# A two-layer hybrid diffusion backbone on one core: the instruction scheduler orders by another estimate of time

## The chip, the cores and the metric

The kernel runs on one core of one Trainium2 chip. The core has five engines with an instruction queue each: TensorE (PE; its weight loads are shown apart as PEld), VectorE (DVE), ScalarE (ACT), GpSimd (POOL) and SyncE (SP), which here issues the loads of weights. The metric is the device time of one execution in microseconds (us), lower is better. The kernel before took 2425.48 us as the median of three runs (2423.67 to 2432.31).

## The reference

256 latent tokens and 256 context tokens of width 1024 go through two layers. Each layer has a mixer of three parallel branches (a Mamba-2 state-space branch in both directions, here SSD; a neighbourhood attention; a Conformer convolution), merged by gates, and a feed-forward part, dense in the first layer and with the best two of eight experts in the second. Both parts are modulated by vectors (adaLN) that are products of a conditioning vector with `ada_w`. All data are float32. Cut to its core:

```
for layer in range(2):
    mod_l = split(silu(c) @ ada_w[layer] + ada_b[layer], 6)       # mod_c from c_ctx
    h_l = modulate(rms_norm(x, norm_mix[layer]), mod_l[0], mod_l[1])
    h_c = modulate(rms_norm(ctx, norm_mix[layer]), mod_c[0], mod_c[1])
    y_l, y_c = token_mixer(h_l, h_c, lp, need_ctx)
    x = x + mod_l[2] * y_l
    h_l = modulate(rms_norm(x, norm_ffn[layer]), mod_l[3], mod_l[4])
    ...
    f_all = swiglu(h_all, ...) if layer == 0 else moe_swiglu(h_all, ...)
    x = x + mod_l[5] * f_all[:, n_ctx:]
return rms_norm(x, final_norm)

def ssd_scan(xs, dt, a, bm, cm, h0):                     # chunks of 128 positions
    decay = exp(where(lower, cs_t[..., :, None] - cs_t[..., None, :], -inf))
    y_diag = einsum('bcgls,bcgels,bcsgep->bclgep', scores, decay, xd)
    y_off = einsum('bclgn,bcgepn,bclge->bclgep', cm, h_in, exp(cs))
    return y_diag + y_off, h_last
```

## The kernel before

**Weights.** Every matrix comes in units of 128x1024 floats (512 KB). `raw` (L119) loads one on SP's queue. `split` makes two numbers of each weight for PE: ACT copies it to a shorter format (L114, the tile h_...), DVE subtracts that from the original (L115, the tile l_...). The activations are split in the same way, and a product is the sum of three, h by H, h by L and l by H (L179, L180, L181 in `wstat`; L226 to L228 in `wmov`). In the mixers three raw buffers and two of each split turn, in the expert loop six and three.

**The mixers** (`mix`). A loop goes over the parts `glu dt qkv xbc g1 ssd p1 g2 p2 z g0 p0` (layer 1: z before p2). g0 to g2 are the gates (tiles wg), z the SSD's gate (zL), p0 to p2 the projections of the branches (wb0ssd_out, wb0na_out, wb0conf_out). Other jobs run in the background: attention, the convolution, the SSD, and the adaLN blocks. They are Python generators; after each weight unit `pump` lets each of them emit some instructions, at a rate. So weight matmuls (fillers) lie in the source between the short steps of these jobs.

**The SSD's end** (`ssd_y`, `ssd_norm`). For a chunk and half of the heads, four groups: `cbS` (L975, PE turns four columns), ACT makes the decays `MS` of it (L978, L979), DVE masks them (L980), PE multiplies (`ydS`, L983). Then `peS` and `yoS` (L996, L997), ACT and DVE on `ES` (L1000 to L1005), and `uL` (L1008). At the end of a layer eight products with z (L932), squares (L934), row sums on PE (`rcyS`, L779), the reciprocal (`rryS`, L787 on DVE, L788 on POOL) and its broadcast on PE (`rbyS`, L791).

**adaLN on DVE** (`ada_v`). 20 blocks; for each, eight tiles `adaw` of 128x512 are loaded on SP (L339) into two buffers and multiplied and summed on DVE (`adac`, L343 for the first, L345 for the others, once or twice for each tile). PE sums over the partitions (`ada`, L350), DVE adds the bias (L351). The twelve blocks of layer 1 run beside the dense feed-forward part of layer 0.

**The experts** (`moe`, `expert`, `stream`). Eight experts, gate and up (eg, eu) and down (ed); r in a name (egr, eur, edr) marks the stream of the sorted tokens. Which expert is next SP reads from memory (L1340), a count from L1224. In the second half two experts' streams run in turn. After each 512 columns a short transpose (L1354) and ACT and DVE steps follow.

**What sets the order.** The instructions of all engines are emitted by the source and then put in order by the scheduler of the tile framework, before the program is compiled: it runs over the instructions with an estimate of when each engine is free and when its inputs are ready, and takes what is ready by priority. The source shifts priorities: `prio` wraps work into `high_priority` with the offsets of `PR` (weights 10000, evacuations, attention, SSD and adaLN 5000, norms 20000, start 30000, `lg` -20000). Each engine then works through its own list in order. The framework is entered in `kernel`, at L1573:

## Time and profile before

| | |
|---|---|
| median of three runs | 2425.48 us (2423.67 to 2432.31) |
| the profiled execution | 2422.2 us, span 2420.4 us |
| granted TensorE clock, mean of the span | 0.988 |
| PE busy, PEld busy | 2317.3 us (96%), 1807.8 us (75%) |
| DVE busy, ACT busy | 1852.8 us (77%), 1338.4 us (55%) |
| loaded by DMA | 469.68 MB, mean 194 GB/s; 326 to 357 GB/s in the expert loop |
| L115 `l_eur`, `l_edr`, `l_egr` on DVE | 154 each, 1.22 us |
| L345 `adac` on DVE | 224, 0.75 us; 54.8 us idle before it |

Busy times are of one engine; times of several overlap. Matmuls are pipelined, so each is shown longer than the distance to the next one. In the table of stretches a row gives, for a stretch, the busy time and number of instructions of each engine, the granted clock, the share of time in which the DMA engines are busy and what they move. A line of waits gives the engine and line that waited, what ended the wait, the sum, the number and the longest. The span falls roughly into the start and layer 0 (to about 1000 us), layer 1's mixers (to about 1560) and the experts (to about 2390).

### The profile page before, as it was taken

How to read it: one execution, taken by the hardware profiler on the slowest of the kernel's cores; microseconds unless marked ns; L12 is line 12 of the kernel's file. 1: busy time of each engine (PE TensorE's matmuls, PEld its weight loads, DVE VectorE, ACT ScalarE, POOL GpSimd, SP SyncE). 2: the span in 40 equal slices, each digit the busy share in tenths (PEclk: the TensorE clock that was granted, in tenths of full speed). 3: DMA queues.
4: the chain of work that ended last, by engine and by line, in shares of the span. 5: the costliest groups of instructions: out<-in, count | busy, mean ns of one | idle time of the engine just before them, and what ended most of it. 6: DMA issues, size and time to landing. Idle time of an engine off the chain costs nothing.

```text
span 2420.4 us, 33213 instructions
## 1 busy us (share of the span) xinstructions
PE 2317.3 (96%) x11647; PEld 1807.8 (75%) x11647; DVE 1852.8 (77%) x2725; ACT 1338.4 (55%) x2048; POOL 22.0 (1%) x30
## 2 busy tenths in 40 slices
PE   7999989999999999999999999899999999999995
PEld 3777757777777777788877899677877787767774
DVE  3669977677766765536889766789898888988986
ACT  3335646654243212225337584487777778788874
POOL 0000000000000000000000000100000000000000
PEclk9999999999999999999999999899999999999998
DMA  7222223234534555433322334399999999999994
GB/s 276 89 75 87 87 66 103 79 100 128 172 104 153 171 186 187 135 99 104 123 87 96 97 114 140 105 352 349 348 335 357 345 326 335 348 327 332 340 334 173
DMA packets 144334, 469.68 MB, mean 194 GB/s; under 512 B 15760, under 2 KB 16272, under 8 KB 144144
## 3 DMA queue, kind: packets, MB, share of 16 engines
q1 hardware_dynamic: 143296, 464.71, 55.8%
q10 hardware_dynamic: 848, 2.62, 0.3%
q8 instruction: 97, 1.59, 0.3%
q14 instruction: 93, 0.76, 0.1%
HBM read 466.22 MB, written 1.05 MB: 193 GB/s over the span
## 4 chain that ended last, share of the span: by engine, by line
PE 75%; DVE 12%; DMA 5%; ACT 4%; issue 3%; POOL 0%; SPq 0%; POOLq 0%; DVEq 0%; ACTq 0%
PE eur L1328 7%; PE egr L1328 6%; PE edr L1328 6%; DMA adaw<-in_ada_w_dram 4%; PE wg L179 2%; PE wg L180 2%; PE wg L181 2%; PE eu L1328 2%; PE ed L1328 2%; PE eg L1328 1%; DVE adac L345 1%; PE xbcL L179 1%; PE xbcL L181 1%; PE xbcL L180 1%; PE ydS L983 1%
## 5 line engine op out<-in xcount | busy, mean ns | idle before, releaser
L115 DVE TENSOR_TENSOR l_eur<-r_eur,h_eur 128x1024 fp32r<-128x1024 f32 x154 | 185.7, 1222 | 27.2 <-ACT h_eur L114 26.0
L115 DVE TENSOR_TENSOR l_edr<-r_edr,h_edr 128x1024 fp32r<-128x1024 f32 x154 | 186.6, 1223 | 21.7 <-ACT h_edr L114 16.6
L345 DVE SCALAR_TENSOR_TENSOR adac<-adaw,sc,adac 128x512 f32<-128x512 f32 x224 | 160.8, 747 | 54.8 <-DMA adaw<-in_ada_w_dram 54.3
L115 DVE TENSOR_TENSOR l_egr<-r_egr,h_egr 128x1024 fp32r<-128x1024 f32 x154 | 186.3, 1220 | 12.4 <-ACT h_egr L114 9.8
L114 ACT ACTIVATE h_edr<-r_edr 128x1024 fp32r<-128x1024 f32 x154 | 162.6, 1060 | 52.7 <-PE edr L1328 26.7
L114 ACT ACTIVATE h_egr<-r_egr 128x1024 fp32r<-128x1024 f32 x154 | 162.3, 1059 | 31.6 <-PE eur L1328 19.3
L114 ACT ACTIVATE h_eur<-r_eur 128x1024 fp32r<-128x1024 f32 x154 | 160.8, 1057 | 23.6 <-PE egr L1328 9.7
L1328 PE MATMUL egr<-l_egr,gHp 128*128 128x512 f32 (+1 forms) x336 | 131.4, 393 | 3.6 <-DVE l_egr L115 3.2
L1328 PE MATMUL eur<-l_eur,gHp 128*128 128x512 f32 (+1 forms) x336 | 129.1, 387 | 2.5 <-DVE l_eur L115 2.1
L179 PE MATMUL wg<-hHm,h_wg 128*128 128x512 f32 (+1 forms) x384 | 130.9, 342 | 0.0
L181 PE MATMUL wg<-hHm,l_wg 128*128 128x512 f32 (+1 forms) x384 | 130.2, 342 | 0.0
L180 PE MATMUL wg<-hLm,h_wg 128*128 128x512 f32 (+1 forms) x384 | 130.1, 340 | 0.0
L1328 PE MATMUL egr<-h_egr,gHp 128*128 128x512 f32 (+1 forms) x336 | 125.8, 377 | 1.1 <-ACT h_egr L114 1.1
L1328 PE MATMUL edr<-l_edr,hHr 128*128 128x512 f32 x308 | 123.4, 401 | 3.3 <-DVE l_edr L115 2.0
L1328 PE MATMUL eur<-h_eur,gHp 128*128 128x512 f32 (+1 forms) x336 | 125.4, 376 | 0.7 <-ACT h_eur L114 0.7
L1328 PE MATMUL edr<-h_edr,hHr 128*128 128x512 f32 x308 | 121.4, 394 | 0.0
L528 DVE SCALAR_TENSOR_TENSOR ccv<-cu,cols,ccv 128x492 f32<-128x492 f32 (+14 forms) x120 | 86.0, 730 | 1.0
L1328 PEld LDWEIGHTS egr<-l_egr,gHp 128*128 128x128 f32 x336 | 63.1, 188 | 27.8 <-DVE l_egr L115 18.6
L1328 PEld LDWEIGHTS eur<-l_eur,gHp 128*128 128x128 f32 x336 | 63.2, 188 | 27.4 <-DVE l_eur L115 17.8
L114 ACT ACTIVATE h_wg<-r_wg 128x1024 fp32r<-128x1024 f32 x48 | 50.7, 1057 | 54.7 <-PE wg L180 35.9
L179 PEld LDWEIGHTS wg<-hHm,h_wg 128*128 128x128 f32 x384 | 72.7, 189 | 9.6 <-issue 2.2
L180 PEld LDWEIGHTS wg<-hLm,h_wg 128*128 128x128 f32 x384 | 72.7, 189 | 9.0 <-issue 2.0
(661 smaller groups left out, 6512.1 us busy)
## 6 DMA issues: line engine op xcount, KB each, us to landing
r_egr<-in_moe_gate_dram SPq DMA_DIRECT2D x154, 512.0 KB, 5.2
r_eur<-in_moe_up_dram SPq DMA_DIRECT2D x154, 512.0 KB, 5.3
r_edr<-in_moe_down_dram SPq DMA_DIRECT2D x154, 512.0 KB, 5.1
adaw<-in_ada_w_dram SPq DMA_DIRECT2D x160, 256.0 KB, 3.1
r_wg<-in_w_in_dram SPq DMA_DIRECT2D x48, 512.0 KB, 3.5
r_xbcL<-in_w_in_dram SPq DMA_DIRECT2D x24, 512.0 KB, 3.5
r_fg<-in_ffn_gate_dram SPq DMA_DIRECT2D x22, 512.0 KB, 3.5
r_fu<-in_ffn_up_dram SPq DMA_DIRECT2D x22, 512.0 KB, 3.5
```

The costliest lines, as they stand in the source:

```text
L114: nc.scalar.activation(Hd, src, AF.Copy)
L115: nc.vector.tensor_tensor(Ld, src, Hd.bitcast(F32), op=ALU.subtract)
L179: mm(out, wh, xh, start=(first and kk == 0), stop=False, skip_group_check=True)
L180: mm(out, wh, xl, start=False, stop=False, skip_group_check=True)
L181: mm(out, wl, xh, start=False, stop=(kk == kc - 1), skip_group_check=True)
L345: nc.vector.scalar_tensor_tensor(d, w, c, d, op0=ALU.mult, op1=ALU.add)
L528: nc.vector.scalar_tensor_tensor(y[:, :, a:b], x[:, :, a + s:b + s], w[:, k:k + 1], y[:, :, a:b], op0=ALU.mult, op1=ALU.add)
L983: nc.tensor.matmul(pd[64 * (i % 2):64 * (i % 2) + 64, (hl // 2) * 128:(hl // 2 + 1) * 128], xd[r][:, hl * 64:(hl + 1) * 64], M[:, i, :], s ...
L1328: mm(ps[j][:, :n], st[kk], w[p][:, k, :], start=(kk == 0 and q == 0), stop=(kk == kc - 1 and q == len(ops) - 1), skip_group_check=True)
```

## The change

One argument is added where the framework is entered. With it the scheduler takes the times by which it orders from a simulated timeline of the program (all engines, queues and transfers advanced together) instead of its simple model, which charges an estimate for each instruction. Priorities, jobs, rates, buffers and every instruction of the source stay as they are:

```
-    with tile.TileContext(nc) as tc:
+    with tile.TileContext(nc, schedule_with_timeline_sim=True) as tc:
         tile_kernel(tc, a, out)
```

The same instructions stand in another order on each engine. Three places of PE's list follow.

**The end of the SSD in layer 0.** PE, from the transposes `cbS` of one step to the product `ydS` that waits for ACT and DVE; zL are weights of the SSD's gate, ada the sum over an adaLN block. Before:

```order
L975 MATMUL cbS_3916<-con_t,cs_669 128x128 x4
L179 MATMUL zL_1_4168<-hHm_254,h_zL_1_4216 128x512
L180 MATMUL zL_1_4168<-hLm_256,h_zL_1_4216 128x512
L181 MATMUL zL_1_4168<-hHm_254,l_zL_1_4217 128x512
L179 MATMUL zL_2_4169<-hHm_254,h_zL_1_4216 128x512
L180 MATMUL zL_2_4169<-hLm_256,h_zL_1_4216 128x512
L181 MATMUL zL_2_4169<-hHm_254,l_zL_1_4217 128x512
```

In the changed order, from the same `cbS`:

```order
L975 MATMUL cbS_3916<-con_t,cs_669 128x128 x4
L983 MATMUL ydS_3915<-MS_3921,xdS_3911 64x128
L975 MATMUL cbS_3932<-con_t,cs_669 128x128
L350 MATMUL ada_3952<-adac_3469,con_t 32x512
L975 MATMUL cbS_3932<-con_t,cs_669 128x128
L350 MATMUL ada_3952<-adac_3469,con_t 32x512
L975 MATMUL cbS_3932<-con_t,cs_669 128x128 x2
L983 MATMUL ydS_3915<-MS_3921,xdS_3911 64x128 x3
L975 MATMUL cbS_3999<-con_t,cs_669 128x128 x4
```

The 13 zL matmuls between `cbS` and its `ydS` have gone from here to an earlier place; from the first `cbS` of the last chunk to `rbyS` 19 weight matmuls are left of 235.

**The adaLN sums in the dense feed-forward part.** PE around the first block of layer 1; fg are its gate products, hTf turned tokens, mrf the modulation spread to all rows. Before:

```order
L181 MATMUL fg_2_5731<-hHf_5571,lfg_0_5736 128x256
L179 MATMUL fg_2_5731<-hHf_5571,hfg_1_5741 128x256
L180 MATMUL fg_2_5731<-hLf_5573,hfg_1_5741 128x256
L181 MATMUL fg_2_5731<-hHf_5571,lfg_1_5742 128x256
L179 MATMUL fg_2_5731<-hHf_5571,hfg_1_5741 128x256
L350 MATMUL ada_6056<-adac_5807,con_t 32x512 x2
L180 MATMUL fg_2_5731<-hLf_5573,hfg_1_5741 128x256
```

In the changed order:

```order
L488 MATMUL hTf_5695<-con_t,xnf_5674 128x128 x4
L450 MATMUL mrf_5709<-mod_4404,con_t 128x512
L450 MATMUL mrf_5712<-mod_4404,con_t 128x512
L450 MATMUL mrf_5715<-mod_4404,con_t 128x512
L450 MATMUL mrf_5718<-mod_4404,con_t 128x512
L350 MATMUL ada_6056<-adac_5807,con_t 32x512 x2
L179 MATMUL fg_0_5729<-hHf_5572,hfg_3_5753 128x256
L180 MATMUL fg_0_5729<-hLf_5574,hfg_3_5753 128x256
```

The block's sum now stands at another point of the gate products, and the sums that follow it stand closer to one another.

**The two streams in the second half of the experts.** PE where the stream edr begins; eur, edr are sorted tokens, eg the other expert, etr a short transpose. Before:

```order
L1328 MATMUL eur_0_19091<-h_eur_1_19108,gHp_16530 128x256
L1328 MATMUL eur_0_19091<-l_eur_1_19109,gHp_16530 128x256
L1328 MATMUL edr_0_19132<-h_edr_0_19135,hHr_18249 128x512
L1328 MATMUL edr_0_19132<-l_edr_0_19136,hHr_18249 128x512
L1328 MATMUL edr_0_19132<-h_edr_0_19135,hHr_18249 128x512
L1328 MATMUL edr_0_19132<-l_edr_0_19136,hHr_18249 128x512
L1354 MATMUL etr_19122<-con_t,eur_19120 128x128 x2
L1328 MATMUL eg_0_18998<-h_eg_2_19145,gH_16873 128x512
```

In the changed order:

```order
L1328 MATMUL eur_0_19091<-h_eur_0_19094,gHp_16530 128x256
L1328 MATMUL eur_0_19091<-l_eur_0_19095,gHp_16530 128x256
L1328 MATMUL eur_0_19091<-h_eur_1_19108,gHp_16530 128x256
L1328 MATMUL edr_0_19132<-h_edr_0_19135,hHr_18249 128x512
L1328 MATMUL eur_0_19091<-l_eur_1_19109,gHp_16530 128x256
L1328 MATMUL eur_0_19091<-h_eur_1_19108,gHp_16530 128x256
```

The first product with h of edr now stands among the products of eur, and its first product with l comes after the rest of eur and two of eg.

## Rows read from the trace of the kernel before

**Rows 1.** The page: its head, and the chain that ended last, by engine.

```profile
span 2420.4 us, 33213 instructions
PE 75%; DVE 12%; DMA 5%; ACT 4%; issue 3%; POOL 0%; SPq 0%; POOLq 0%; DVEq 0%; ACTq 0%
```

**Rows 2.** Timeline of PE: start, duration, engine, line, operation, out<-in, shape.

```profile
640.16 0.39 PE L180 MATMUL wb0ssd_out<-yS0L,h_wb0ssd_out 128*128 128x512 f32 x1
640.39 0.39 PE L181 MATMUL wb0ssd_out<-yS0H,l_wb0ssd_out 128*128 128x512 f32 x1
```

**Rows 3.** Stretches: PE, PEld, DVE, ACT, POOL busy (instructions), clock, DMA.

```profile
240.00:300.00 60.00, 59.81 (x264) 44.77 (x262) 57.84 (x105) 36.89 (x61) 0.00 (x0) 1.00 0.28 88
300.00:360.00 60.00, 51.29 (x224) 33.17 (x225) 46.91 (x86) 26.29 (x56) 0.00 (x0) 0.94 0.23 69
```

**Rows 4.** Timeline of PE at both ends of the SSD tails, layers 0 and 1.

```profile
493.88 0.64 PE L975 MATMUL cbS<-con_t,cs 128*128 128x128 f32 x4
...
582.34 0.65 PE L791 MATMUL rbyS<-con_t,rryS 128*128 128x128 f32 x4 [0.77 <-POOL rryS L788]
...
1435.52 0.65 PE L975 MATMUL cbS<-con_t,cs 128*128 128x128 f32 x4
...
1466.65 0.43 PE L791 MATMUL rbyS<-con_t,rryS 128*128 128x128 f32 x2
```

**Rows 5.** Groups of DVE, 494 to 582 us: busy, mean ns, idle before.

```profile
L345 DVE SCALAR_TENSOR_TENSOR adac<-adaw,sc,adac 128x512 f32<-128x512 f32 x30 | 20.9, 748 | 0.0
...
L980 DVE TENSOR_TENSOR MS<-MS,scmS 128x512 f32<-128x512 f32 x8 | 5.3, 689 | 1.8 <-ACT MS L979 1.8
```

**Rows 6.** Timeline of DVE in the tails of layer 0 and layer 1.

```profile
570.38 0.75 DVE L345 SCALAR_TENSOR_TENSOR adac<-adaw,sc,adac 128x512 f32<-128x512 f32 x1
571.05 0.69 DVE L932 TENSOR_TENSOR uL<-uL,zL 128x512 f32<-128x512 f32 x1
...
580.58 0.16 DVE L787 TENSOR_SCALAR rryS<-rcyS 128x4 f32<-128x4 f32 x1 [2.04 <-PE rcyS L779]
...
1456.62 0.69 DVE L1001 TENSOR_TENSOR ES<-ES,yoS 128x512 f32<-128x512 f32 x1 [3.25 <-ACT ES L1000]
```

**Rows 7.** Who waited for L980, 300 to 494; what L983 waited for, 1380 to 1470.

```profile
  PEld ydS L983: 10.7, 5
  PE ydS L983: 9.2, 2
...
  DVE MS L980: 1.2, 5
```

**Rows 8.** Timeline of DVE: four of layer 1's twelve L351, first and last among them.

```profile
759.88 0.68 DVE L351 TENSOR_TENSOR mod<-ada,mod 32x512 f32<-32x512 f32 x1 [1.28 <-PE ada L350]
...
939.89 0.68 DVE L351 TENSOR_TENSOR mod<-ada,mod 32x512 f32<-32x512 f32 x1 [0.85 <-PE ada L350]
...
958.79 0.68 DVE L351 TENSOR_TENSOR mod<-ada,mod 32x512 f32<-32x512 f32 x1 [1.14 <-PE ada L350]
...
998.64 0.70 DVE L351 TENSOR_TENSOR mod<-ada,mod 32x512 f32<-32x512 f32 x1
```

**Rows 9.** Waits from 1980 to 2390: sum, number, longest.

```profile
PEld edr L1328 <- DVE l_edr L115: 10.3, 19, 1.0
...
PEld egr L1328 <- DVE l_egr L115: 9.7, 19, 1.0
PEld eur L1328 <- DVE l_eur L115: 8.5, 20, 0.8
...
PEld esr L1354 <- ACT esr L1366: 5.0, 10, 0.9
```

**Rows 10.** The page: two of the costliest groups, busy and mean ns.

```profile
L115 DVE TENSOR_TENSOR l_edr<-r_edr,h_edr 128x1024 fp32r<-128x1024 f32 x154 | 186.6, 1223 | 21.7 <-ACT h_edr L114 16.6
...
L114 ACT ACTIVATE h_edr<-r_edr 128x1024 fp32r<-128x1024 f32 x154 | 162.6, 1060 | 52.7 <-PE edr L1328 26.7
```

**Rows 11.** SP's reads of the expert numbers: ns min/median/max, first, last.

```profile
L1340 SPq TENSOR_LOAD <-eidi x8: 265/270/465, 1568.3 to 1995.1; - x8
```

**Rows 12.** A stretch of half clock, columns as in rows 3.

```profile
351.90:358.70 6.80, 5.02 (x20) 3.75 (x21) 5.09 (x9) 2.60 (x9) 0.00 (x0) 0.50 0.39 107
```

## The prediction

> **What bounds the kernel now.** The page comes first: its chain of what ended last is three quarters TensorE (PE), one eighth VectorE (DVE) [rows 1]. PE's busy share cannot be used as a fill level, because one 128x512 matmul is shown 0.39 us long while the next starts 0.23 us later [rows 2]. So I read the table of stretches by the number of matmuls: 60 us with 264 of them have a PE that hardly waits, 60 us with 224 have lost some 9 us or more, at a granted clock of 0.94 [rows 3]. The time goes down only where such waits go, and up where a reordering opens new ones; the arithmetic itself is the same, since the same instructions run. The profiled execution took 2422.2 us (span 2420.4), 3.3 us less than the median 2425.48; I sum against 2422.2 and add 3.3 at the end.
>
> I compared the two orders on every engine, and asked of each stretch: how much PE work lies there, against the chain that has to end in it. Four places matter.
>
> **1. Tail of the layer-0 SSD.** From the `cbS` product at 493.88 to the `rbyS` product at 582.34 PE needs 88.5 us before [rows 4]. In that place 235 weight matmuls stand in before's order and 19 in after's: 216 x 0.23 us [rows 2] = 49.7 us of cover have left, so the tail would shrink to 38.8 us if nothing else set its length. But DVE, which works strictly in its order, does there the SSD's own steps and the adaLN products. In after's order 67 DVE instructions lie between the first `MS` (L980) and `rryS` (L787): 26 `adac` at 748 ns and 8 `MS` at 689 ns [rows 5] are 19.4 and 5.5 us, the rest, of the same kinds as elsewhere, 21.8; together 46.7 us of durations. Back to back, each starts about 0.08 us before the last has ended (570.38 + 0.75 against 571.05) [rows 6], so 46.7 - 67 x 0.08 = 41.3 us. To that come waits which no filler hides any more: the last row sums (2.0 us before `rryS`) and from there to `rbyS` 1.8 us (580.58 to 582.34) [rows 4, 6], and the wait of L1001 for ACT, 3.3 us in the row of layer 1 [rows 6], twice. Sum 51.7 us, against 38.8: **+13** us. Not all of it is lost: the 216 matmuls now stand in earlier SSD steps and cover waits there. Of the waits of `ydS` for `MS` before the tail, PE lost 9.2 us and its weight loads 10.7 [rows 7], at most 19.9 together if they do not overlap. Between nothing and 19.9 I take half, since the fillers reach most steps but 15 of 48 have less than 3 us between `cbS` and `ydS` (6 in before): -9.5. Term **+3.5** (from -7 to +13). If the cover in the earlier steps turns out useless, the price is the +13.
>
> **2. Tail of the layer-1 SSD.** The same place in layer 1 took 1435.52 to 1466.65 = 31.1 us [rows 4]. All 156 weight matmuls (half as wide, so 0.12 us by halving rows 2: 18.7 us) leave it; 12.4 us remain. DVE there: 26 instructions, 12.5 us less 26 x 0.08 = 10.4, and 3.3 + 2.0 + 1.8 as above = 17.5. So +5.1, and only 1.2 us of `ydS` waits to win back [rows 7]. Term **+4** (0 to +8, the top if both waits on ACT stand bare).
>
> **3. The adaLN blocks of layer 1 in the feed-forward part.** Twelve blocks of eight `adaw` tiles, through two buffers, are multiplied on DVE (L345) and summed by two or one matmul (L350). Before, the twelve results (L351) lie between 759.88 and 998.64 [rows 8]: 238.8 us for eleven intervals, 21.7 on average; the fastest blocks take 18.5 to 18.9 us (939.89 to 958.79 is one of four) [rows 8], and that the floor is met four times says it is the ring's own pace. The PE work between the first and the last L350 falls from 226 to 196 us, since they stand closer in the new order (worked out by 0.23 us for each 512-wide matmul and half for each 256-wide one). At 18.7 us for an interval that has less work than that, and the work for the others, the eleven need 206 to 213 us, 10 to 17 more than their work; before they needed 238.8 - 226 = 13, of which some 5 were waits of other kinds. Those 5 come on top. Term **+6** (0 to +13): the ring cannot run further ahead, because SP issues the next tile when a buffer is free. What DVE loses by waiting for a tile is hidden only as long as PE has matmuls in front of L350.
>
> **4. Second half of the expert loop.** From about 1980 us two experts' streams alternate, each weight tile is split by ACT into h (1.06 us) and by DVE into l (1.22 us) [rows 10], and three buffers turn. PE's weight loads wait there for l tiles, 10.3, 9.7 and 8.5 us in the three largest rows, and the short transposes L1354 for ACT, 5.0 us for `esr` [rows 9]. In each order I took, tile by tile, the PE work from the last use of a buffer to the first use of the l tile that comes into it. It needs the two durations and the releases between, 2.75 us. What is short of that sums to 44.5 us before (the l waits of [rows 9] with the smaller ones are 43) and to 27.9 us after: -16.6. The transposes now have weight matmuls ahead of them: up to -9. Against it, the order now puts h products in front of the other stream's group, and what the h tiles are short of 1.6 us rises from 2.8 to 14.3 us: +11.5. The ends are -25 and +8; the middle is -9, and I take **-10**. The first half of the loop keeps its order nearly unchanged.
>
> **Smaller terms.** In the mixers' weight loops all h products of a tile now come before the first l product; the l shortage there falls from 3.7 us to nothing: -2 (-4 to 0). On SP seven loads of the expert numbers and three of the counts move up behind the first expert weights: ten of about 0.27 us, at most 0.47 [rows 11], 3 to 5 us of queue time. SP waits for free buffers there, the weights behind them are six buffers ahead of PE: 0, and at most +1 if the first waits are shorter. The steps of the router that DVE does in another order: 0 (-0.3 to +1.5). New stretches with little PE work bring the clock down: after such a wait it stood at 0.50, the lower of its two levels (1.2 against 2.4 GHz), for 6.8 us [rows 12], which costs at most 3.4 us of PE time and nothing where DVE is the bound; for the two tails between 0 and 6.8, I take +2.5, a little under the middle.
>
> Sum: 2422.2 + 3.5 + 4 + 6 - 10 - 2 + 2.5 = 2426.2; with 3.3 for the median **2429.5**, rounded to 2430.
>
> **The clock, another way.** [Rows 12] show half clock only for a stretch after PE had stood idle, and [rows 3] show 1.00 in 60 us in which DVE was 57.8 us busy and PE had fillers. The Trainium skill, in "TensorE: Matmul & The Clock Gate", section "Part 1: The HAM clock gate", states that the throttled state is the default and that activity releases it; by that rule a tail in which PE mostly waits could stay throttled throughout. No row here shows so long a stretch with half-filled PE. As a mechanism of this kernel: after's tail holds 38.8 us less its old waits of 9, so 29.8 us of PE work; at half clock it is 59.6, 8 more than the 51.7 that DVE needs, and layer 1 gives about 1: +9 in place of +2.5, **2436**.
>
> **The rivals.**
> A. *The tails decide (slower).* The cover moved to earlier steps hides nothing, because those steps wait for ACT's part of `MS`, not for lack of matmuls. Price: +13 in place of +3.5, tail two at +8, and the ring, which runs in the same stretch, at +13: 2429.5 + 9.5 + 4 + 7 = **2450**. It is slower by over 0.5% once these three together exceed the forecast by 8. For it: 15 steps with little cover. Against it: the median cover of a step rises from 5.7 to 7.1 us.
> B. *h first costs more than it gives (slower).* The expert loop ends at +8: **2447.5**. Decides if ACT, which also does the evacuations in the new order, is late with h by over a microsecond at each change of stream.
> C. *The expert loop gives its full -25 and the earlier steps win back 15 of 19.9* (faster): 2429.5 - 15 - 6 - 4 (ring at +2) = **2404.5**; for it, the transposes' waits vanish on paper.
> D. *The new order is one the machine does not feel:* queues and buffers absorb it, every term but the forecast's small ones is nil: **2425**.
>
> **How the numbers follow.** Forecast 0.30, D 0.10, the clock case 0.07; A 0.18, B 0.15; C 0.20. 0.5%, about 12 us, is what a measurement can tell from no change here. The forecast's own terms add to -42 and +44 at their ends, but not all at once; 2416 to 2443 is its own range, and a part of it (0.03 each way) lies past 2413.4 or 2437.6. Faster: C and that part, 0.22. Slower: A, B and that part, 0.35. Same: 0.43. The range from 2400 to 2460 takes in C and A and the bounds of the expert loop and leaves out the cases in which several ends meet.
>
> **What would show it.** Profile after: in the layer-0 tail, from `cbS` (the first with under 20 weight matmuls behind it) to `rbyS`, 50 us or more and DVE full there, PE with 20 us of waits; between the first and last L351 of layer 1 205 to 215 us, with L350 waiting for `adac` 15 us or more; in the second half of the expert loop the l waits at two thirds of [rows 9], waits for h tiles over 10 us, the L1354 waits under 3. The prediction is wrong in step 1 if the tail is under 45 us; in step 4 if the 360 us from 1980 are not between 340 and 368 long for the same matmuls; wholly, if a stretch that I have called unchanged (the start, latent attention, the first half of the experts) moves by over 10 us.

## The result and the profile after

The changed kernel took 2505.47 us (median of four runs, 2504.22 to 2510.47), the kernel before 2426.45 beside it (2423.67 to 2432.31). The ratio is 1.0326, with an interval from 1.0302 to 1.0350: 79 us slower. The forecast was 2430 with a range from 2400 to 2460, so the time lies far outside it. The profiled execution of after took 2506.17 us, that of before 2422.2.

The page of after: its head, TensorE's granted clock in 40 slices, and the chain that ended last, which answer to [rows 1].

```profile
span 2504.3 us, 33214 instructions
...
PEclk9999879998699999999999899889999999999998
...
PE 80%; DVE 8%; ACT 5%; DMA 4%; issue 2%; POOL 0%; SPq 0%; DVEq 0%; ACTq 0%; POOLq 0%
```

DVE's share of the chain is 8 % after 12 %, PE's 80 % after 75 %. Read by itself this looks like a kernel that waits less. It is not: PE is busy 2347.9 us after 2317.3, with the same products, and its clock over the span has gone from 0.988 to 0.961. A PE that runs at half clock is shown busy longer for the same products (below, eight transposes 1.94 us instead of 1.08), so a chain of waits that ends on PE can hide what was lost by a wait a few microseconds earlier.

To find the place, the two traces are laid side by side at points by which PE has done the same work in both orders: the first transpose `btS` of the SSD (L875), the first product of the SSD's projection (`wb0ssd_out`, and `wb1ssd_out` in layer 1), the last L226 product of the dense feed-forward part (`fd`), and the `pos` product with which the experts' sorting ends (L1146). These are rows by line and tile, with duration in ns (least, median, most) and the first and last start in us. Of before:

```profile
L875 PE MATMUL btS<-con_t,uL x16: 272/273/328, 332.8 to 1368.3; 128*128 128x128 f32 x16
L179 PE MATMUL wb0ssd_out<-yS0H,h_wb0ssd_out x64: 388/389/792, 626.4 to 678.9; 128*128 128x512 f32 x64
L226 PE MATMUL fd<-hfd,f2H x24: 388/389/481, 1112.2 to 1131.2; 128*128 128x512 f32 x24
L179 PE MATMUL wb1ssd_out<-yS1H,h_wb1ssd_out x64: 283/283/283, 1501.1 to 1523.8; 128*128 128x256 f32 x64
L1146 PE MATMUL pos<-emask,onesr x1: 353/353/353, 1564.9 to 1564.9; 128*128 128x16 f32 x1
```

And of after:

```profile
L875 PE MATMUL btS<-con_t,uL x16: 271/273/476, 365.0 to 1471.1; 128*128 128x128 f32 x16
L179 PE MATMUL wb0ssd_out<-yS0H,h_wb0ssd_out x64: 389/389/796, 693.9 to 747.1; 128*128 128x512 f32 x64
L226 PE MATMUL fd<-hfd,f2H x24: 389/389/478, 1180.3 to 1197.8; 128*128 128x512 f32 x24
L179 PE MATMUL wb1ssd_out<-yS1H,h_wb1ssd_out x64: 280/283/357, 1609.6 to 1632.3; 128*128 128x256 f32 x64
L1146 PE MATMUL pos<-emask,onesr x1: 350/350/350, 1671.8 to 1671.8; 128*128 128x16 f32 x1
```

From these rows (the fourth of each list by its first start, `fd` by its last) and the two spans:

| stretch | before, us | after, us | difference |
|---|---|---|---|
| start and both attentions of layer 0, to `btS` | 332.8 | 365.0 | +32.2 |
| SSD of layer 0 and its norm, to `wb0ssd_out` | 293.6 | 328.9 | +35.3 |
| to the end of the dense feed-forward part | 504.8 | 503.9 | -0.9 |
| mixers of layer 1, to `wb1ssd_out` | 369.9 | 411.8 | +41.9 |
| to `pos` | 63.8 | 62.2 | -1.6 |
| experts and end | 855.5 | 832.5 | -23.0 |
| sum | 2420.4 | 2504.3 | +83.9 |

So both mixers lose, and the experts give back about a fifth of it. The next question is what PE waited for. Its waits in the mixers of layer 0, before (140 to 700 us):

```profile
PE ydS L983 <- DVE MS L980: 9.2, 2, 4.7
PE PT L690 <- DVE P L687: 2.7, 4, 1.5
```

After (140 to 748 us):

```profile
PE PT L690 <- DVE P L687: 18.3, 5, 7.8
PE wg L179 <- ACT g L637: 12.9, 4, 7.4
PE ada L350 <- DVE adac L345: 7.6, 2, 6.1
PE ydS L983 <- DVE MS L980: 5.7, 3, 2.6
```

The largest row is new: the transposes of attention's probabilities (`PT`, L690) wait for the softmax on DVE (the tile `P`, ended at L687). Three of these transposes in PE's timeline of after, with the idle time before them in brackets:

```profile
303.91 1.30 PE L690 MATMUL PT<-con_t,P 128*128 128x128 f32 x5 [7.81 <-DVE P L687]
...
317.41 1.08 PE L690 MATMUL PT<-con_t,P 128*128 128x128 f32 x8 [0.48 <-DVE P L687]
...
361.22 1.94 PE L690 MATMUL PT<-con_t,P 128*128 128x128 f32 x8 [4.04 <-DVE P L687]
```

Eight transposes take 1.08 us in the second row and 1.94 in the third: the clock has fallen. The stretches of after, columns as in [rows 3], tell where: attention's end, the last 50 us of the SSD's tail, the way from `rbyS` to `wb0ssd_out`.

```profile
300.00:366.00 66.00, 46.43 (x143) 25.10 (x144) 28.59 (x80) 22.02 (x64) 0.00 (x0) 0.68 0.07 20
...
607.00:658.00 51.00, 38.09 (x157) 24.56 (x155) 38.88 (x66) 13.99 (x33) 1.01 (x1) 0.63 0.28 79
658.00:694.00 36.00, 28.65 (x107) 20.09 (x106) 29.69 (x45) 13.42 (x20) 0.00 (x0) 0.81 0.40 124
```

In the first of them no engine is near full and the weights' DMA stands nearly still: 143 matmuls in 66 us, where [rows 3] have 224 and 264 in 60. This is a chain that runs bare, and the reason stands on DVE 80 us earlier. The softmax of the first latent head (half of it) on DVE, before:

```profile
189.68 0.42 DVE L703 TENSOR_TENSOR P<-S,bt 128x256 f32<-128x256 f32 x1 [0.40 <-PE S L699]
...
194.70 0.16 DVE L710 TENSOR_TENSOR st<-st 128x2 f32<-128x2 f32 x1
```

And after; L528 are taps of the convolutions, which belong to other jobs:

```profile
222.35 0.42 DVE L703 TENSOR_TENSOR P<-S,bt 128x256 f32<-128x256 f32 x1
...
225.96 1.41 DVE L528 SCALAR_TENSOR_TENSOR cvL<-uL,cols,cvL 128x510 f32<-128x510 f32 x2
...
237.44 0.15 DVE L710 TENSOR_TENSOR st<-st 128x2 f32<-128x2 f32 x1
```

The same steps take 15.1 us instead of 5.0, and the view shows no wait of DVE among them: other work stands between them. In DVE's lists 65 instructions with 28 taps stand from the first head's first L703 to its last PT copy (L692) before, 104 with 61 taps after. The three heads that follow then have few instructions between their steps, since most taps are used up, and PE has few fillers: by PE's start-to-start times in the trace of before, the products `po` of the four heads stood at 191, 218, 265 and 289 us of PE work, and stand at 260, 269, 279 and 289 now. Three heads have to run through in the last 29 us of PE work, one after the other, and that is the 66 us stretch.

The dt path of the SSD (L819 to L841 on DVE) shows the same hand: before, mostly with one tap between two steps, it went from 94.81 to 117.90, after, mostly with two, from 95.72 to 137.96. What stands between the same two steps, L829 and L830, in before and then in after:

```profile
104.28 0.75 DVE L528 SCALAR_TENSOR_TENSOR ccv<-cu,cols,ccv 128x510 f32<-128x510 f32 x1
```

```profile
110.80 1.40 DVE L528 SCALAR_TENSOR_TENSOR ccv<-cu,cols,ccv 128x510 f32<-128x510 f32 x2
```

One tap is enough to hide the step's own delay on the chip: L830 starts at 104.94 in before and at 112.12 in after, in both with no wait shown ahead of it. The second only pushes the chain back. The new order stands as if a result came out later than it does.

### The profile page after: what moved, and what is told of

Read it like the earlier page. It is cut to its first block, busy times and chain, and to the rows that moved or that the text cites. A ratio compares the mean times of both kernels' runs of the same rounds, so it can differ in the third digit from the quotient of the medians.

```text
span 2504.3 us, 33214 instructions
## 1 busy us (share of the span) xinstructions
PE 2347.9 (94%) x11647; PEld 1851.1 (74%) x11647; DVE 1850.1 (74%) x2725; ACT 1341.4 (54%) x2052; POOL 20.4 (1%) x30
## 4 chain that ended last, share of the span: by engine, by line
PE 80%; DVE 8%; ACT 5%; DMA 4%; issue 2%; POOL 0%; SPq 0%; DVEq 0%; ACTq 0%; POOLq 0%
PE egr L1328 7%; PE eur L1328 7%; PE edr L1328 6%; DMA adaw<-in_ada_w_dram 3%; PE wg L179 2%; PE wg L180 2%; PE wg L181 2%; PE eg L1328 2%; PE eu L1328 2%; PE ed L1328 2%; PE xbcL L181 2%; PE xbcL L179 2%; PE xbcL L180 2%; PE fd L226 2%; DVE adac L345 2%
## 5 line engine op out<-in xcount | busy, mean ns | idle before, releaser
L181 PE MATMUL wg<-hHm,l_wg 128*128 128x512 f32 (+1 forms) x384 | 119.8, 346 | 1.8 <-DVE l_wg L115 1.8
L115 DVE TENSOR_TENSOR l_wg<-r_wg,h_wg 128x1024 fp32r<-128x1024 f32 x48 | 58.6, 1222 | 51.9 <-ACT h_wg L114 51.7
L978 ACT ACTIVATE MS<-cbS,cs 128x128 f32<-128x128 f32 x192 | 55.1, 387 | 57.3 <-PE cbS L975 57.2
L528 DVE SCALAR_TENSOR_TENSOR ccv<-cu,cols,ccv 128x482 f32<-128x482 f32 (+14 forms) x120 | 83.4, 729 | 0.0
```

Source lines behind the costliest of these rows:

```text
L115: nc.vector.tensor_tensor(Ld, src, Hd.bitcast(F32), op=ALU.subtract)
L181: mm(out, wl, xh, start=False, stop=(kk == kc - 1), skip_group_check=True)
L528: nc.vector.scalar_tensor_tensor(y[:, :, a:b], x[:, :, a + s:b + s], w[:, k:k + 1], y[:, :, a:b], op0=ALU.mult, op1=ALU.add)
L978: nc.scalar.activation(M[:, i, :], pb[:, i * 128:(i + 1) * 128], AF.Relu, bias=cs[:, b, r, h0 + i:h0 + i + 1], scale=-1.0)
```

## The experiments

The first theory: the whole loss lies in the order of the mixers, the experts' gain is independent of it, and losses of single stretches add. Its sharper form said that PE's list decides. The rival theories said that the lists of ACT and DVE decide, or that the half clock is the loss itself. An order is fixed in these kernels by a table that names, for an engine, which instruction follows which; each pair gets a dependency for the scheduler alone, with no wait on the chip. What the table doesn't name the new scheduler orders as it likes. The diffs stand against the changed kernel, unless something else is said; the table itself is left out. The ratios are each against the kernel before on the same chip, where its medians were between 2423.95 and 2427.11.

**The mixers in the old order** (all engines, everything ahead of the experts; the new scheduler orders the rest):

```
+PINS = [('PE', 7258), ('ACT', 1081), ('DVE', 1930), ('POOL', 25), ('SP', 450)]
...
+def pin(tc):
...
+                tc.add_manual_dep(ins[rank], prev.name, mybir.DependencyInfo(mybir.DependencyClass.NoSync, mybir.DependencyReason.DATA), reason="pin")
...
     Body(ctx, tc, a, out, dbg, stop).run()
+    pin(tc)
```

> All instructions traced before the expert loop stand, on every engine, in the order of the kernel before (fixed by order-only dependencies from a table); the expert loop keeps the order of the changed kernel. Theory 1 (the new order loses in the mixers alone, because matmuls that cover the short chains are used up early, and gains in the expert loop): the trace of the changed kernel lost 101 us up to the first expert product and won 22 from there, so this is 2426 - 22 = 2404, within 4, and faster than both. Theory 2 (the shorter expert loop only takes back work that was done ahead of it, or follows from the mixers' late end): 2422 to 2430.

Measured: 2404.54 us (2400.47 to 2407.94), ratio 0.9903 [0.9881, 0.9924]. It beats before by 1 % and after by 4 %, as the first theory said. Its `pos` row, to be held against the two above:

```profile
L1146 PE MATMUL pos<-emask,onesr x1: 350/350/350, 1570.8 to 1570.8; 128*128 128x16 f32 x1
```

The span of this run is 2406.2, so 835.4 us lie behind `pos`, after 855.5 before and 832.5 in the changed kernel. Up to `pos` it is 6 us behind before, where the changed kernel is 107 behind (the expectation's 101 and 22 us are 107 and 23 by the rows above). So the loss is in the order ahead of the experts, the experts' gain of 20 us stays without it, and both are shown by one run.

**Attention alone, and the SSD alone, in the old order** (in layer 0, what the engines do there; the first table is attention's, the SSD's is the same with `[('PE', 1256), ('ACT', 276), ('DVE', 341)]`):

```
+PINS = [('PE', 1275), ('ACT', 214), ('DVE', 463)]
...
+    pin(tc)
```

> In the changed kernel PE, ACT and DVE go through everything up to the end of layer 0's latent attention in the order of the kernel before; the PE work ahead of each later step of the SSD is the same as in the changed kernel. Theory 1 (each stretch of short steps without weight matmuls pays for itself): the 38 us of the bare attention come back and the 35 of the SSD and its norm stay: 2505 - 38 = 2467, within 8. Rival (what the attention saves is lost again in the SSD, whose own waits grow, since it is the same DVE work that is late): 2490 or more.

> In the changed kernel PE, ACT and DVE go through layer 0's SSD (from the first turn of B to the first product of the SSD's projection) in the order of the kernel before; the attention ahead of it stays bare. If the losses of the stretches add up: 2505 - 25 - 10 = 2470, within 8, and together with the run that undid the attention the two make up the 73 us of layer 0. If the SSD's loss comes from being started late by the attention: 2490 or more.

Measured: attention 2473.93 us, ratio 1.0194 [1.0167, 1.0221]; SSD 2477.86, ratio 1.0226 [1.0205, 1.0246]. Both lie in the ranges expected, near their upper ends. Against the kernel before beside them they give back 32 and 25 us of the 79. The first `btS` and the first `wb0ssd_out` with attention in the old order:

```profile
L875 PE MATMUL btS<-con_t,uL x16: 271/272/476, 334.4 to 1435.4; 128*128 128x128 f32 x16
...
L179 PE MATMUL wb0ssd_out<-yS0H,h_wb0ssd_out x64: 387/389/501, 658.3 to 713.0; 128*128 128x512 f32 x64
```

And with the SSD in the old order:

```profile
L875 PE MATMUL btS<-con_t,uL x16: 271/273/476, 365.9 to 1441.1; 128*128 128x128 f32 x16
...
L179 PE MATMUL wb0ssd_out<-yS0H,h_wb0ssd_out x64: 388/389/799, 661.1 to 714.8; 128*128 128x512 f32 x64
```

From `btS` to `wb0ssd_out` these are 323.9 and 295.2 us, against 293.6 before and 328.9 after. So attention's order costs 31 us ahead of `btS` and 5 behind it, the SSD's costs 34 us behind it and nothing ahead; together they are the 67.5 us that layer 0 lost up to `wb0ssd_out`, and there the two parts add. Of the 34 us some 6 are lost again later in the run (1816.7 us from `wb0ssd_out` to the end of its span of 2477.8, 1810.4 in after); where wasn't followed. The mixers of layer 1 had no run of their own: that their 42 us have the same causes is read from the trace alone (PE waits there for `PT` 9.3 us, after 0.8).

**Some engines' lists at a time** (PE's; the other two are the same with `[('DVE', 1930)]` and with `[('ACT', 1081), ('DVE', 1930), ('POOL', 25)]`):

```
+PINS = [('PE', 7258)]
...
+    pin(tc)
```

> In the changed kernel PE alone goes through all that comes before the expert loop in the order of the kernel before; ACT, DVE and SP keep the new scheduling. Theory 1 (the place of the weight matmuls on PE decides): 2404 to 2412, near the run with all engines in the old order. Rival (the lists of DVE and ACT decide: the first latent head has 61 convolution taps between its steps on DVE instead of 28, and here still 47): 2440 or more.

> In the changed kernel DVE alone goes through all that comes before the expert loop in the order of the kernel before. Theory 2 with DVE as the list that decides: 2405 to 2425. If ACT's list is at fault as well: 2440 or more.

> The other half of the run with PE in the old order: in the changed kernel ACT, DVE and POOL go through all that comes before the expert loop in the order of the kernel before, and PE is free under the new scheduling. Theory 2 (new, after the run with only PE in the old order came out at 2557: the lists of DVE and ACT are at fault, since they put long-ready convolution taps between the steps of a chain, and PE's fillers only follow the late chain): 2404 to 2420. Theory 1 (PE's own choice of weight matmuls over chain steps loses by itself): 2440 or more.

Measured: PE's list 2556.86 us, ratio 1.0536 [1.0509, 1.0563]; DVE's 2604.70, 1.0749 [1.0728, 1.0771]; DVE, ACT and POOL 2587.45, 1.0678 [1.0653, 1.0704]. All three are slower than after itself, so "PE's list decides" and "the lists of ACT and DVE decide" fall alike, as long as each means that one side put back would be enough. The waits of PE over the whole span with PE's old list show what happens:

```profile
PE cs L846 <- DVE dtA L841: 37.3, 2, 24.0
PE PT L690 <- DVE P L687: 27.9, 7, 6.9
```

PE comes to the SSD's sums and to the transposes at the old point, and DVE still spreads its chains over taps. With DVE's old list it is the other way round; the largest wait of PE in the mixers of layer 0 is then one for a split:

```profile
PE xbcL L181 <- DVE l_xbcL L115: 17.7, 6, 7.7
```

In these three runs a list taken from one schedule and put into the other came out worse than either schedule whole. How much of the loss began on which engine they can't tell, since the mixture itself costs time.

**The mixers' weight products in the order of the source**, on PE (the two helpers also serve the dense feed-forward part, so its products are held as well):

```
-        mm = self.nc.tensor.matmul
+        mm = lambda *a, **k: self.tc.keep_in_program_order(self.nc.tensor.matmul(*a, **k))
```

> In the changed kernel the mixers' weight matmuls are held on PE behind everything that the source emits ahead of them, so a filler cannot be taken before the chain's step that stands ahead of it in the source. Theory 1: the four latent heads are evenly spread again, so the bare stretches go; but PE now waits where the source's rate of steps is too high. 2400 to 2450. Rival (the source's order makes PE wait for every step): above 2505.

Measured: 2705.95 us, ratio 1.115 [1.1121, 1.118]; PE waits at each step of the chains, here over the whole span:

```profile
PE PT L690 <- DVE P L687: 82.5, 14, 13.5
PE cs L846 <- DVE dtA L841: 68.5, 2, 36.9
```

That the fillers have left the source's order is thus not the fault by itself; with this scheduler the source's order is far worse.

**Taps between the softmax's steps, in the kernel before.** All lists as before; only on DVE 33 taps of the conformer, which stood behind the first latent head, are moved between the steps of its softmax, two at most of them. The diff is against before, the moved taps are in the table:

```
+PINS = [('PE', 7258), ('ACT', 1081), ('DVE', 1930), ('POOL', 25), ('SP', 450)]
...
     Body(ctx, tc, a, out, dbg, stop).run()
+    pin(tc)
...
     with tile.TileContext(nc) as tc:
```

> The kernel before, its order held on every engine, but for one thing: 33 of the Conformer's convolution taps (L528, 0.65 us each from start to start), which DVE does after the first latent head of layer 0, stand two by two behind the steps of that head's softmax, as the changed kernel puts such taps. The sums and their order stay the same. If taps between the steps of a chain cost time, though DVE does no more in all: the chain of this one head grows by up to 33 x 0.65 = 21 us, PE has only its old cover and waits: 8 to 21 us slower, 2432 to 2446. If they are harmless because DVE is the bound there and gets the work out of the way: 2424 within 4.

Measured: 2447.43 us (2445.64 to 2449.39), ratio 1.0099 [1.0082, 1.0116]: 23.4 us for 33 x 0.65 = 21 us of taps, which DVE has to do in any case. All of it is lost ahead of the SSD: the first `btS` comes at 358.2, after 332.8. The softmax then runs from 190.83 (L703) to 207.07 (L710), 16.2 us after 5.0, much as in the changed kernel, and the waits of PE (140 to 760 us) show the same new row as after's:

```profile
PE PT L690 <- DVE P L687: 20.5, 4, 15.3
```

So taps between the steps of one short chain are enough to lose over a quarter of what the change lost, with nothing else moved. Here PE's list was held, so the wait falls on PE in one piece of 15.3 us; in after PE's list had made room, and the loss came at the end of the heads. The opposite, the taps taken out of the changed kernel's own lists, was not run.

**The clock held up in the changed kernel.** All lists as after; 13 products of no use, 128x512, stand on PE ahead of the three transposes that wait 7.8, 5.6 and 4.0 us:

```
+                    for _ in range(FILL.get(f"{nm}{j}{qb}", 0)):
+                        FILLER.append(mm(pt, self.con("id"), self.con_t[:, 0:512], start=True, stop=True, skip_group_check=True).ins)
...
+FILL = {"0256100": 6, "0256201": 4, "0256301": 3}
```

> The changed kernel in its own order on every engine, with 13 added matmuls of about 1 us each whose results are overwritten: 6, 4 and 3 of them ahead of the three transposes of layer 0's latent attention for which PE waited 7.8, 5.6 and 4.0 us. They do no useful work; they keep PE busy where it waits. If the lower clock after these waits is part of the loss (some 14 us of PE work in that stretch is done at half speed that the kernel before did at full): 8 to 14 us faster than the changed kernel, 2491 to 2497. If the loss is the waits for DVE and ACT alone: 2505 within 3, or slower by what sticks out.

Measured: 2497.86 us (2493.36 to 2502.58), ratio 1.0315 [1.0298, 1.0332], which does not differ from after's 1.0326 by more than the intervals; the time lies between the two expectations. In the trace the effect is there, in the stretch of 0.68 above and in the first `btS` (L877 here, since two lines were added):

```profile
300.00:366.00 66.00, 51.85 (x199) 27.67 (x199) 34.89 (x92) 23.72 (x67) 0.00 (x0) 0.92 0.07 22
```

```profile
358.50 0.44 PE L877 MATMUL btS<-con_t,uL 128*128 128x128 f32 x2
```

The clock rises to 0.92 and `btS` comes at 358.5 instead of 365.0: 6.5 us of the 32, a little under what was expected. (Of the 199 matmuls shown, 26 are the 13 added products, which are shown as two each; the others are the kernel's own, which came sooner.) So in attention the clock is a consequence that makes the loss larger, not its cause; in the SSD it was not raised.

**Attention and SSD at a higher priority in the changed kernel**:

```
-    PR = dict(w=10000, ev=5000, conv=0, att=5000, ssd=5000, ada=5000, norm=20000, init=30000, lg=-20000)
+    PR = dict(w=10000, ev=5000, conv=0, att=40000, ssd=40000, ada=5000, norm=20000, init=30000, lg=-20000)
```

> The changed kernel with the priority offsets of attention and SSD raised from 5000 to 40000, far above the weights' 10000. If the offsets decided, the chains would be drawn ahead and the kernel would come to 2450 or less. If the new scheduler goes by when a step is ready and the offset only breaks ties: 2505 within 10; the PE work ahead of the four latent heads of layer 0 hardly moves in the order.

Measured: 2522.34 us, ratio 1.0410 [1.0389, 1.0431], 17 us slower than after and outside the 10 that were expected. The four heads' products stand at 258, 269, 279 and 289 us of PE work, as in after. So the taps do not stand between the steps because of a higher priority. That fits an order in which a step is not yet ready when the tap is taken; it doesn't say which of the scheduler's estimates makes it late, and that stays open.

## Why the prediction was wrong, point by point

**Left out: latent attention.** This is the step that failed most: 53 of the 84 us had no term. The sum has four places, all chosen by asking where cover leaves a chain; attention in both layers was taken as unchanged, and the text named it as what would make the forecast wholly wrong if it moved by over 10 us. Layer 0 lost 32 us up to `btS`. In layer 1 PE's time over its own work from the first latent product to `btS` went from 8.6 to 29.3 us: 21 more. The view that would have shown it was at hand before: the same question of PE work against the chain, put to `po` of each head (191 to 289 us before, 260 to 289 after), and the number of taps between the first L703 and the last L692. I looked at the end of each chain for missing cover, and not at its head for foreign work.

**Step 1, the tail of the layer-0 SSD.** The tail was mis-sized. Its two ends in after, the first `cbS` of the last chunk (19 weight products stand behind it) and `rbyS`, which answer to [rows 4]:

```profile
592.43 0.60 PE L975 MATMUL cbS<-con_t,cs 128*128 128x128 f32 x4
...
657.61 0.69 PE L791 MATMUL rbyS<-con_t,rryS 128*128 128x128 f32 x2
```

They are 65.2 us apart, where 51.7 was worked out: 26 over the 38.8 us of PE work, not 13. DVE's own work was as worked out, 46.5 us of durations from the first `MS` to `rryS`. Its waits were not. From 592 to 658 us DVE waited 21 us: 4.4 for ACT's part of `MS`, 4.4 for PE's `xtyS`, 5.4 for PE's `ada`, 4.7 for `adaw` tiles and some more. The sum had 6.6 for L1001, which was 1.3, and 2.0 ahead of `rryS`, which was nothing; and it left out the 2.5 us from `cbS` to the first `MS`. Two of the waits that it did not have:

```profile
602.93 1.90 DVE L980 TENSOR_TENSOR MS<-MS,scmS 128x512 f32<-128x512 f32 x3 [3.45 <-ACT MS L979]
...
615.98 0.88 DVE L343 TENSOR_SCALAR adac<-adaw,sc 128x512 f32<-128x512 f32 x2 [2.91 <-PE ada L350]
```

The credit for the earlier steps failed as well. The waits of `ydS` did fall, from 10.7 and 9.2 [rows 7] to 3.9 and 3.1 us between 366 and 607; in their place stand `wg` for ACT's `g` (3.9 us), `peS` for `MS` and `repS` (4.7) and many short stops. PE's time over its own work from `btS` to `rbyS` went from 38.8 to 63.8 us: +25, and the tail alone makes that up, so the earlier steps won back about nothing where -9.5 stood in the sum. And the way from `rbyS` to `wb0ssd_out` had no term at all: it lost 10 us, 7.4 of them in one wait. The 19 weight products of the tail had all been done by 597 us, and on DVE the first step of the norm (L942, at 660.61) stood behind an `adac` that had waited for its tile:

```profile
667.92 0.80 PE L179 MATMUL wg<-hHm,h_wg 128*128 128x512 f32 x1 [7.35 <-ACT g L637]
...
669.37 0.63 PE L179 MATMUL wg<-hHm,h_wg 128*128 128x512 f32 x1
```

The first products after the wait are shown at 0.63 us and from 672 on at 0.39, so the clock was late as well. Of rival A ("the tails decide", 2450) the mechanism held, the cover in the earlier steps was worth nothing net, and the adaLN ring, which A alone had in this stretch, is among the waits; A's price of 13 for the tail was half of what it cost.

**Step 2, the tail of layer 1.** It took 22.9 us (the sixteenth `cbS` ahead of `rbyS` at 1564.86, `rbyS` at 1587.79), where 17.5 was worked out: 10.5 over its 12.4 us of PE work, not 5.1. The SSD of layer 1 and its norm lost 19 us over PE's own work (14.3 and 4.6), of which the tail is about 10; the term was +4.

**Step 3, the adaLN blocks.** The distance was right and the sign wrong. The twelve L351 of layer 1 in after, which answer to [rows 8]:

```profile
L351 DVE TENSOR_TENSOR mod<-ada,mod x12: 672/688/697, 821.2 to 1025.5; 32x512 f32<-32x512 f32 x12
```

First to last are 204.3 us; 206 to 213 were forecast, against 196 us of work, so 8 us over it, where 13 were over it before. The feed-forward part gained 0.9 us instead of losing 6. The working had set 5 us of other waits on top and they went instead: DVE waits 2.0 us for `ada` ahead of an L351 in that stretch, after 14.5 before, and PE no longer waits for `adac` there (7.3 before).

**Step 4, the expert loop.** The mechanism was right and the size under what came. Waits of after from 2085 to 2475 us, the stretch of [rows 9]:

```profile
PEld ed L1328 <- ACT h_ed L114: 6.8, 16, 0.7
...
PEld edr L1328 <- DVE l_edr L115: 4.1, 6, 1.5
...
PEld eur L1328 <- DVE l_eur L115: 2.1, 6, 0.6
...
PEld egr L1328 <- DVE l_egr L115: 1.0, 3, 0.4
...
PEld etr L1354 <- ACT eur L1381: 0.4, 2, 0.2
```

The l waits of the sorted stream fell from 28.5 us [rows 9] to 7.2, not to two thirds; h waits rose to over 20 us, where the forecast had over 10; the transposes' waits vanished. PE's time over its own work in the second half went from 48.5 to 32.6 us (-16, for -10), and the first half, called nearly unchanged, from 17.8 to 11.8 (-6). Rival B (h first costs more than it gives) is refuted, and rival C was right about the loop. That the run with the old mixers came to 2404.5, C's number for the whole, is luck: C got it with 10 us from the SSD's steps and the ring, which that run leaves as they were before, and a forecast that stood 4 us above before.

**The clock.** The term was +2.5 for two tails, from a stretch of 6.8 us [rows 12]. The granted clock was at 0.68 for 66 us at attention's end, 0.63 in the last 50 us of the tail and 0.81 behind it. The clock case of the prediction had reckoned with a tail at half clock throughout, 59.6 us long; the tail took 65.2, so that case came nearer than the forecast's 51.7, and neither had the waits named in step 1. What the clock cost in the tail is not shown, since no run raised it there. It stood in the chain: DVE waited 5.4 us for `ada`, and the 64 row sums `rcyS`, 0.11 us from start to start in before, followed one another by 0.21, 48 of them in one piece:

```profile
643.89 10.40 PE L779 MATMUL rcyS<-con_t,ysqS 128*128 128x1 f32 x48
```

They end at 654.29 and `rryS` starts at 654.73; but the `adac` ahead of it on DVE, late by its tiles, ended at 654.70, so faster sums alone would not have brought `rryS` forward. The Trainium skill says in "TensorE: Matmul & The Clock Gate", section "Part 1: The HAM clock gate", that the throttled state is the default and that activity releases it. The traces agree: 0.68 where PE had 143 matmuls in 66 us, and 0.92 there with the 13 added products. In attention, where PE's chain was bare, the clock cost 6.5 us by these two traces.

**The sum.** The terms that stood in it came to +4 on 2422.2; by the same places they measured 35.3 for the SSD of layer 0 with its norm, 19 for that of layer 1, -0.9 for adaLN and -23 for the experts, +30 together. The 53 us of attention in both layers (32 and 21) had no term. With 1 us of small change this is the +84 of the spans. Two slips of the working change nothing here: the low ends of its terms add to -40, not -42, and by its own list of chances faster, same and slower come to 0.23, 0.41 and 0.36, not 0.22, 0.43 and 0.35.

## What to carry to other kernels

When a reordering is judged, ask two things of every chain of short dependent steps, and of all of them: how much cover its end still has, and how much long-ready work now stands between its first steps on the engine that does them; in the one run that moved nothing else, the second was paid in full (33 taps of 0.65 us cost 23.4 us), and in the changed kernel it showed later as missing cover somewhere else. A scheduling option need not be taken whole: the stretch where it wins can be kept and the rest held by order-only dependencies, here on all engines of the stretch at once (2404.5 us, against 2426 and 2505); held on PE alone, or on DVE with or without ACT and POOL, it came out at 2557 to 2605. And a chain of waits that ends more on PE than before is no sign of a fuller PE as long as the granted clock isn't read beside it.

## What the runs showed of the hardware

Two things were not expected. Thirteen products of no use made the stretch that held them shorter: the granted clock there went from 0.68 to 0.92, eight transposes took 1.08 us instead of 1.94, and the chain ended 6.5 us earlier. And a dependent step on DVE costs little more than an independent one: three such steps of before follow one another by 0.72 us (1457.34, 1458.06, 1458.79 in DVE's timeline) where an instruction that doesn't need the result starts 0.60 later (495.00, 495.59), so about 0.1 us is all that a filler between them could hide.
